# First norm of a decoder layer summed without passes between, and ten modulation blocks at other places of the order

## The chip, the cores and the metric

The kernel runs on one core of a Trainium2 chip. The metric is the device time of one execution in microseconds, as a median of several runs. Times inside an execution are read from a profile of one execution; they count from the start of its span. The engines are named as in the profile: PE is the matmul engine (TensorE), PEld its weight loads, DVE the vector engine, ACT the scalar engine, POOL GpSimd, and SP the engine from whose queue the loads of this kernel are issued (SPq).

## What is computed

One layer of a hybrid decoder, for 256 tokens of width 1024, in float32. A vector `c` gives six modulation vectors; the token mixer (attention of 8 heads beside an SSD group of 16 heads) and a convolutional FFN follow, each behind an RMS norm:

```python
mod = jax.nn.silu(c) @ w_ada[l] + b_ada[l]
shift1, scale1, gate1, shift2, scale2, gate2 = (
    m[:, None, :] for m in jnp.split(mod, N_MOD, axis=-1))
h = rms_norm(x, norm1_g[l]) * (1 + scale1) + shift1
x = x + gate1 * hybrid_token_mixer(h, ...)
h = rms_norm(x, norm2_g[l]) * (1 + scale2) + shift2
x = x + gate2 * conv_ffn(h, ...)
```

In the mixer one projection of `h` gives q, k, v, z, x/B/C and dt. q and k are normed for each head; the attention is causal softmax over the 256 tokens; the SSD group is one chunk of 256 with its decays, a skip and a gate by `silu(z)`. Each group's output is normed, and one output projection takes both.

## The kernel before

**Matmuls.** A weight chunk of 128 rows arrives as `raw` and is split into a high part `whi` (L189, mostly ACT) and a low part `wlo` (L191, mostly DVE). An activation has such parts too (`hhi` and `hlo`, `yhi` and `ylo`, `ahi` and `alo`). A product is then three matmuls: high by high, low weight by high, high weight by low activation. These are L419 in the first stage, L828 to L830 in the stage of z, q, k and v, and L345 to L347 in the output projection and the FFN. L826 multiplies an unsplit chunk.

**The first norm.** Eight tiles `sq` of squares are summed over the features by one-column matmuls against `ones` (L276, two halves of the tokens each, into bank 7; the matmul of a float32 tile shows as two passes in the trace). The square root (ACT, L279) and the reciprocal (DVE, L281) follow, and two transposes (L300) lay the factors along the row that `hbuf` (L385) multiplies. `hhi` (L392) and `h` (L394) come from that, and then the first L419. `keep_warm` (L305) multiplies `ones` by `ones` into a bank that nobody reads; it stands between the sums (`fill`), behind them and behind the transposes. `between()` is `modulate1`: the first two modulation blocks on DVE.

**Modulation.** The product with `w_ada` is made of 48 blocks: each is a load `ada` of 512 KB and, for blocks 0 to 39, one multiply with a running sum on DVE (`ada_dve`, L246). For blocks 16 to 39 the list `ada_u`, sorted, gives the unit of work at which a block stands. It sets two places at once, that of the block's load in SP's queue (behind weight chunk unit + 4) and that of its L246:

```python
ada_unit = sorted(P["ada_u"])
ada_after = [N1 + u + P["ada_lead"] for u in ada_unit] + ...
...
for i in range(16, 40):
    u = ada_unit[i - 16]
    put(u, ada_dve, i)
```

Three `ada` tiles go round for these blocks, so a load waits in the queue until the block three before it has been used, and what stands behind it in SP's queue waits too.

**Units.** A unit is a weight chunk of the second part of the kernel: 0 to 4 are z, 5 to 28 q, k and v, 29 to 44 the output projection. At fixed units stand the conv and dt work, the SSD heads (`ssd_y`: L602 and L603 on PE for a pair of heads, then L604 and L606 on DVE; the decays `m` are L584 to L591), the q and k norms (`rqk` L290 to L296, `qk` L662, transposes L668, `kT` L674), the attention heads (scores L683 and L684, softmax L689 to L705, transposes L711 to L713, the product with v L719 and L720, its parts `ahi` L722 and `alo` L724), the sums for the norms of the groups (L611) and the normed SSD output (`hbuf` L629, `yhi` L630, `ylo` L631).

**Order.** The order of SP is the one written. On PE, DVE and ACT a scheduler with costs of its own orders the instructions from the units, so a change of the list moves many others. Each of these engines then works through its list as it stands: an instruction that waits holds up what is behind it on its engine.

Of the kernel before, what the change touches and what calls it, by code (L numbers as in the profile page):

```python
# [16 lines left out]
D = 1024  # L17
# [24 lines left out]
V_DTB = 326  # L42
V_ALL = 327

P = {'n2l': 6, 'sqa': 0, 'xr0': 0, 'scp': 1, 'vq': 1, 'v1': 6, 'n2': 4, 'hpx': [1, 0, 1, 0, 0, 1], 'e0': 0, 'ev': [1, 0, 1, 0], 'ada_u': [3, 4, 5, 5, 6, 7, 10, 9, 9, 19, 20, 20, 22, 24, 24, 25, 33, 35, 36, 37, 39, 39, 41, 42], 'ada_e': [1, 1, 1, 1, 1, 1, 1, 1, 1, 1, 1, 1, 1, 1, 1, 1, 1, 1, 1, 1, 1, 1, 1, 1], 'ada_lead': 4, 'ada_s': 0, 'g2': 68, 'hip': [0, 0, 0, 0, 0, 0, 0, 0, 0, 0, 0, 0, 0, 0, 0, 0, 0, 0, 0, 0, 0, 0, 0, 0, 0, 0, 0, 0, 0, 0, 1, 0, 0, 0, 1, 0, 0, 0, 0, 1, 0, 0, 0, 0, 0, 0, 0, 0, 0, 0, 0, 0, 0, 0, 0, 0, 0, 0, 0, 0], 'conv': [0, 0, 1, 0, 2, 5, 5, 4, 8, 4, 7, 6], 'dt': [1, 2, 2, 4], 'cdb': [7, 7], 'xbt': [9, 12, 11, 12], 'Y0': 14, 'DL': 3, 'ab0': 11, 'ss': 9, 'so': 2, 'qk': [12, 14, 17, 20, 21, 23], 'A0': 21, 'so1': 2, 'so2': 3, 'pv0': 26, 'sm_e': [0, 0, 1, 0, 1, 0, 0, 0], 'dc_e': [2, 2, 2, 0, 2, 2, 2, 0, 2, 2, 2, 0, 2, 2, 2, 0], 'mm_e': [1, 1, 1, 1, 1, 1, 1, 1, 1, 1, 1, 1, 1, 1, 1, 1], 'gz_e': [0, 0, 0, 0, 0, 0, 0, 0], 'sq_e': [1, 1, 1, 1, 1, 1, 1, 1], 'final': 2, 'ab_q': 0, 'LA': 2, 'asu': 34, 'aru': 38, 'aod': 2, 'w0': 4, 'w1': 4, 'w2': 4, 's1la': -1, 'zi': 1, 'lop': [0, 0, 0, 0, 0, 0, 0, 0, 0, 0, 0, 0, 0, 0, 0, 0, 0, 0, 0, 0, 0, 0, 0, 0, 0, 0, 0, 0, 0, 0, 0, 0, 0, 0, 0, 0, 0, 0, 0, 0, 0, 0, 0, 0, 0, 0, 0, 0, 0, 0, 0, 0, 0, 0, 0, 0, 0, 0, 0, 0], 'subs': [2, 1, 1, 1, 1, 1, 1, 1, 1, 1, 1, 1, 1, 1, 1, 1], 's1a': [0, 1, 0, 1, 0, 0, 0, 0]}

@with_exitstack
def mixer_ffn(ctx: ExitStack, tc: tile.TileContext, xT_d, c_d, vec_d, alog_d, ada_d,
# [22 lines left out]
    bank = [ps.tile([128, 512], F32, name=f"bank{i}") for i in range(8)]  # L71


    RAW, HL, ADA, LA = 8, 5, 3, P["LA"]
# [162 lines left out]
    sq8 = T([128, KT, S], "sq8", tag="big_x")  # L237
# [33 lines left out]
    def rms_sum(parts, n, pb, between=lambda: None, fill=None):  # L271
        for i, p in enumerate(parts):
            if fill and i % 2:
                keep_warm(fill, bank[2][:, 0:128])
            for t in range(2):
                pe.matmul(pb[:, t:t + 1], p[:, t * 128:(t + 1) * 128], ones[:, 0:1], start=(i == t == 0),  # L276
                          stop=(i == len(parts) - 1), skip_group_check=True)
        r = rt()
        act.activation(r[:, 2:4], pb[:, 0:2], AF.Sqrt, bias=epsc, scale=1.0 / n)  # L279
        between()  # L280
        dve.reciprocal(r[:, 0:2], r[:, 2:4])  # L281
        return r
# [15 lines left out]
    def rms_transpose(r, pb):  # L298
        for t in range(2):
            i = pe.transpose(pb[:, 256 + t * 128:384 + t * 128], r[:, t:t + 1].to_broadcast([128, 128]), ident)  # L300
        return i

    def keep_warm(n, out):
        for _ in range(n):
            pe.matmul(out, ones, ones, start=True, stop=True)  # L305
# [30 lines left out]
        ada_dve(1)  # L336

    keep_warm(4, bank[2][:, 0:128])
    r1 = rms_sum([sq8[:, kt] for kt in (0, 1, 2, 3, 4, 6, 5, 7)], D, bank[7], modulate1, 1)
    keep_warm(2, bank[2][:, 0:128])  # L340
    rms_transpose(r1, bank[7])
    keep_warm(5, bank[2][:, 0:128])

    def mm3(out, w, h, start, stop):
        pe.matmul(out, w[0], h[0], start=start, stop=False, skip_group_check=True)  # L345
# [85 lines left out]
    for kt in range(KT):  # L431
        if kt == 0:
# [5 lines left out]
            w0 = get(0)  # L438
# [310 lines left out]
    Y0, DL = P["Y0"], P["DL"]  # L749
# [21 lines left out]
    A0 = P["A0"]  # L771
# [40 lines left out]
    for j in range(6):  # L812
        m, hf = divmod(j, 2)
        bs = (bank[4], bank[6]) if j % 2 else (bank[5], bank[7])
        for q4 in range(4):
# [3 lines left out]
            for k2 in range(2):  # L819
                kt = q4 * 2 + k2 + (m == 2)  # L820
# [244 lines left out]
```

## Time and profile before

| | us |
|---|---|
| median of the runs | 430.8 (430.69, 430.8, 431.64) |
| profiled execution | 430.68 |
| its span, first to last instruction | 429.0 |
| PE busy | 422.5 |
| DVE busy | 344.4 |
| ACT busy | 268.2 |
| POOL busy | 26.0 |

The profiled execution is 1.7 us longer than its span. The busy time of an engine is a sum over the whole span. PE's waits and the timeline of a stretch say where something is late: a row of a timeline has the start, the duration, the engine, the line, the operation, output and inputs, the count of instructions that it holds, and, where the engine stood idle before it, how long and for what. Durations of matmuls overlap, since they are pipelined; the pace of the matmuls is read from one start to the next.

### The profile page before, as it was taken

Reading aid. Unit: us, or ns where it says so; the run is one execution under the profiler, and the core shown is the slowest. Engines: PE = TensorE matmul, PEld = TensorE weight load, DVE = VectorE, ACT = ScalarE, POOL = GpSimd, SP = SyncE. Lnnn points to the kernel's source line nnn. Section 1 sums busy time; section 2 is a strip of 40 time slices with the busy share of each in tenths; the row PEclk is TensorE's granted clock in tenths of the full one; section 3 lists DMA queues with packets and bytes.
Section 4 is the critical chain, followed back from the end, with each engine's and each line's share of the span. In section 5 each row is a group of like instructions: output and inputs, shape, how many; then the busy total and the mean of one; then the engine's idle time right before and its main releaser. Section 6 shows DMA issues by size and latency. Waiting matters only on the chain.

```text
span 429.0 us, 7921 instructions
## 1 busy us (share of the span) xinstructions
PE 422.5 (98%) x3020; PEld 385.1 (90%) x3020; DVE 344.4 (80%) x680; ACT 268.2 (63%) x534; POOL 26.0 (6%) x24
## 2 busy tenths in 40 slices
PE   8999999999999999999999999999999999999996
PEld 8899998768767567889999999999999999999996
DVE  4779968999659888999999699778787877777755
ACT  4375448826999775886267495576666655555640
POOL 2000000000000001000000000222332200000000
PEclk9899999999999999999999999999999999999999
DMA  7999965889359549234691468767776665554002
GB/s 270 398 414 408 388 195 179 306 313 339 103 178 384 185 150 377 100 136 165 232 348 55 136 249 278 270 219 257 261 244 207 236 197 198 161 185 148 0 2 98
DMA packets 29589, 96.19 MB, mean 224 GB/s; under 512 B 3680, under 2 KB 6128, under 8 KB 29552
## 3 DMA queue, kind: packets, MB, share of 16 engines
q1 hardware_dynamic: 29520, 95.68, 62.5%
q8 instruction: 23, 0.38, 0.4%
q14 instruction: 14, 0.11, 0.1%
q10 hardware_dynamic: 32, 0.02, 0.0%
HBM read 94.62 MB, written 1.06 MB: 223 GB/s over the span
## 4 chain that ended last, share of the span: by engine, by line
PE 78%; DVE 9%; DMA 6%; ACT 5%; issue 1%; SPq 1%; ACTq 0%
PE bank L347 17%; PE bank L345 17%; PE bank L346 17%; PE bank L826 4%; PE bank L805 4%; PE bank L828 4%; DMA raw<-in_win_dram 4%; PE bank L829 4%; PE bank L830 4%; DVE wlo L191 2%; DMA vec<-in_vec_dram 2%; ACT whi L189 2%; DVE adax L246 2%; PE bank L931 2%; DVE ada L246 1%; PE bank L419 1%
## 5 line engine op out<-in xcount | busy, mean ns | idle before, releaser
L191 DVE TENSOR_TENSOR wlo<-raw,whi 128x1024 fp32r<-128x1024 f32 (+2 forms) x115 | 143.0, 1245 | 13.8 <-ACT whi L189 13.6
L189 ACT ACTIVATE whi<-raw 128x1024 fp32r<-128x1024 f32 (+2 forms) x112 | 115.0, 1035 | 40.8 <-PE bank L347 30.3
L347 PE MATMUL bank<-h2lo,whi 128*128 128x256 f32 x336 | 95.2, 283 | 0.0
L345 PE MATMUL bank<-h2hi,whi 128*128 128x256 f32 x336 | 95.2, 283 | 0.0
L346 PE MATMUL bank<-h2hi,wlo 128*128 128x256 f32 x336 | 95.1, 283 | 0.0
L916 DVE SCALAR_TENSOR_TENSOR fbuf<-bank,vec,fbuf 128x255 f32<-128x255 f32 (+1 forms) x84 | 40.2, 481 | 30.7 <-ACT fbuf L914 29.3
L347 PEld LDWEIGHTS bank<-h2lo,whi 128*128 128x128 f32 x336 | 64.5, 192 | 0.2 <-DVE h2lo L900 0.2
L345 PEld LDWEIGHTS bank<-h2hi,whi 128*128 128x128 f32 x336 | 64.5, 192 | 0.1
L346 PEld LDWEIGHTS bank<-h2hi,wlo 128*128 128x128 f32 x336 | 64.5, 192 | 0.0
L345 PE MATMUL bank<-fsp,whi 128*128 128x256 f32 x176 | 49.8, 283 | 0.0
L346 PE MATMUL bank<-fsp,wlo 128*128 128x256 f32 x176 | 49.8, 283 | 0.0
L347 PE MATMUL bank<-fsp,whi 128*128 128x256 f32 x176 | 49.8, 283 | 0.0
L914 ACT ACTIVATE fbuf<-bank,vec 128x256 f32<-128x256 f32 x42 | 23.4, 560 | 35.0 <-PE bank L347 35.0
L246 DVE SCALAR_TENSOR_TENSOR ada<-ada,cb 128x1024 f32<-128x1024 f32 x30 | 36.5, 1216 | 0.6 <-DMA ada<-in_ada_dram 0.6
L345 PEld LDWEIGHTS bank<-fsp,whi 128*128 128x128 f32 x176 | 33.8, 192 | 0.0
L346 PEld LDWEIGHTS bank<-fsp,wlo 128*128 128x128 f32 x176 | 33.8, 192 | 0.0
L347 PEld LDWEIGHTS bank<-fsp,whi 128*128 128x128 f32 x176 | 33.8, 192 | 0.0
L828 PE MATMUL bank<-whi,hhi 128*128 128x512 f32 x70 | 29.7, 429 | 0.0
L829 PE MATMUL bank<-wlo,hhi 128*128 128x512 f32 x70 | 28.9, 412 | 0.0
L830 PE MATMUL bank<-whi,hlo 128*128 128x512 f32 x70 | 28.3, 404 | 0.0
L251 POOL TENSOR_TENSOR ada<-ada,cb 128x1024 f32<-128x1024 f32 x8 | 19.8, 2474 | 114.9 <-DMA ada<-in_ada_dram 114.9
L419 PE MATMUL bank<-hhi,whi 128*128 128x256 f32 (+1 forms) x128 | 21.5, 292 | 0.0
(223 smaller groups left out, 830.9 us busy)
## 6 DMA issues: line engine op xcount, KB each, us to landing
raw<-in_wup_dram SPq DMA_DIRECT2D x44, 512.0 KB, 4.3
ada<-in_ada_dram SPq DMA_DIRECT2D x38, 512.0 KB, 5.3
raw<-in_wdn_dram SPq DMA_DIRECT2D x22, 512.0 KB, 3.7
raw<-in_winq_dram SPq DMA_DIRECT2D x16, 512.0 KB, 4.3
raw<-in_wout_dram SPq DMA_DIRECT2D x16, 512.0 KB, 4.7
adax<-in_ada_dram SPq DMA_DIRECT2D x10, 512.0 KB, 9.4
raw<-in_win_dram SPq DMA_DIRECT2D x8, 456.0 KB, 9.8
raw<-in_win_dram SPq DMA_DIRECT2D x7, 512.0 KB, 9.8
```

Source lines behind the costliest of these rows:

```text
L189: act.activation(hi[:, c], t[:, c], AF.Copy)
L191: (pool if lo_on_pool(i) else dve).tensor_tensor(lo[:, c], t[:, c], hi[:, c].bitcast(F32), op=OP.subtract)
L246: dve.scalar_tensor_tensor(t, t, 1.0, sc, op0=OP.mult, op1=OP.mult, accum_out=mod[:, i:i + 1])
L345: pe.matmul(out, w[0], h[0], start=start, stop=False, skip_group_check=True)
L346: pe.matmul(out, w[1], h[0], start=False, stop=False, skip_group_check=True)
L347: pe.matmul(out, w[0], h[1], start=False, stop=stop, skip_group_check=True)
L419: pe.matmul(s1_acc(i)[:m], w[k % 2], h[k // 2], start=(kt == k == 0 and i in (0, 2, 4, 6, 8, 10, 13, 14)), stop=last and kt == KT - 1, ski ...
L828: pe.matmul(bs[t], hhi[:, kt, blk(t)], w[0][:, wc], start=(q4 == k2 == 0), stop=False)
L829: pe.matmul(bs[t], hhi[:, kt, blk(t)], w[1][:, wc], start=False, stop=False)
L830: pe.matmul(bs[t], hlo[:, kt, blk(t)], w[0][:, wc], start=False, stop=(kt == KT - 1))
L914: act.activation(a, src, AF.Identity, bias=vec[:, V_FB + i:V_FB + i + 1], scale=vec[:, w + 2:w + 3])
L916: dve.scalar_tensor_tensor(a[:, s:], src[:, :S - s], vec[:, w + 2 - s:w + 3 - s], a[:, s:], op0=OP.mult, op1=OP.add)
```

## The change

Two edits. In the first norm the sums run without `keep_warm` between them; the two calls behind the sums become seven, and the five behind the transposes become two. In the list `ada_u` (sorted) ten numbers are smaller: blocks 25 to 34 stood at units 19, 20, 20, 22, 24, 24, 25, 33, 35, 36 and now stand at 12, 13, 15, 17, 19, 20, 20, 22, 24, 25; block 35 goes from 37 to 33, block 36 from 39 to 37. Blocks 16 to 24 and 37 to 39 stay.

```diff
-    'ada_u': [3, 4, 5, 5, 6, 7, 10, 9, 9, 19, 20, 20, 22, 24, 24, 25, 33, 35, 36, 37, 39, 39, 41, 42]
+    'ada_u': [3, 4, 5, 5, 6, 7, 9, 9, 10, 12, 13, 15, 17, 19, 20, 20, 22, 24, 25, 33, 37, 39, 41, 42]
...
     keep_warm(4, bank[2][:, 0:128])
-    r1 = rms_sum([sq8[:, kt] for kt in (0, 1, 2, 3, 4, 6, 5, 7)], D, bank[7], modulate1, 1)
+    r1 = rms_sum([sq8[:, kt] for kt in (0, 1, 2, 3, 4, 6, 5, 7)], D, bank[7], modulate1)
+    keep_warm(7, bank[2][:, 0:128])
+    rms_transpose(r1, bank[7])
     keep_warm(2, bank[2][:, 0:128])
-    rms_transpose(r1, bank[7])
-    keep_warm(5, bank[2][:, 0:128])
```

On PE, at the first norm, the last rows of the sums and what follows them (`bank_72` takes the sums and the transposes, `rt` is the square root's tile):

```order
-L276 MATMUL bank_72<-ones,sq_158 128x1 x4
-L305 MATMUL bank_67<-ones 128x128
-L276 MATMUL bank_72<-ones,sq_158 128x1 x2
+L276 MATMUL bank_72<-ones,sq_158 128x1 x16
+L305 MATMUL bank_67<-ones 128x128 x7
+L300 MATMUL bank_72<-ident,rt_173 128x128 x2
 L305 MATMUL bank_67<-ones 128x128 x2
-L300 MATMUL bank_72<-ident,rt_173 128x128 x2
-L305 MATMUL bank_67<-ones 128x128 x5
```

All 16 sums stand in a row, and seven passes of `ones` instead of two stand between them and the transposes.

On DVE, in the q and k part, where the low half of chunk `whi_83` is made (`wlo_88`). `bank_68` holds the result of L602 and L603 for a pair of SSD heads. Before:

```order
L290 TENSOR_SCALAR nw_178<-ssq 128x24
L606 TENSOR_TENSOR xsT<-xsT,zs 128x256
L191 TENSOR_TENSOR wlo_88<-raw_77,whi_83 128x1024
L315 TENSOR_TENSOR accg_788<-accg_788,sq_172 128x256
L291 TENSOR_SCALAR nwi<-nw_178 128x24
L191 TENSOR_TENSOR wlo_89<-raw_79,whi_84 128x1024
L292 TENSOR_SCALAR rqk<-nwi 128x24
L604 SCALAR_TENSOR_TENSOR xsT<-xsT,vec,bank_68 128x256
```

and after:

```order
L290 TENSOR_SCALAR nw_178<-ssq 128x24
L291 TENSOR_SCALAR nwi<-nw_178 128x24
L292 TENSOR_SCALAR rqk<-nwi 128x24
L294 TENSOR_TENSOR nw_179<-rqk 128x24
L295 SCALAR_TENSOR_TENSOR nw_179<-nw_179,nw_178 128x24
L604 SCALAR_TENSOR_TENSOR xsT<-xsT,vec,bank_68 128x256
L191 TENSOR_TENSOR wlo_88<-raw_77,whi_83 128x1024
L315 TENSOR_TENSOR accg_786<-accg_786,sq_172 128x256
```

L604 stood five rows behind `wlo_88` and now stands right ahead of it. On PE the same place reads after the change:

```order
L602 MATMUL bank_68<-m_784,xdt 64x256
L603 MATMUL bank_68<-m_784,xdt 64x128
L828 MATMUL bank_69<-whi_83,hhi 128x512
L828 MATMUL bank_71<-whi_83,hhi 128x512
L829 MATMUL bank_69<-wlo_88,hhi 128x512
L830 MATMUL bank_69<-whi_83,hlo 128x512
```

The pair of heads whose L603 ends two matmuls ahead of the first use of `wlo_88` is the one that L604 above waits for; before, three L828 stood between.

On PE, at the start of the output projection, the second L719 (second head) and what is ahead of it. Before:

```order
L347 MATMUL bank_69<-ylo,whi_85 128x256
L345 MATMUL bank_70<-yhi,whi_82 128x256
L346 MATMUL bank_70<-yhi,wlo_87 128x256
L347 MATMUL bank_70<-ylo,whi_82 128x256
L711 MATMUL bank_67<-ident,p_1463 128x128
L719 MATMUL bank_68<-pT_798,vS 128x256
L720 MATMUL bank_68<-pT_798,vS 128x128
```

and after, with the first L345 of the kernel in the first row:

```order
L345 MATMUL bank_70<-yhi,whi_82 128x256
L683 MATMUL bank_65<-kT,qT 128x128
L684 MATMUL bank_65<-kT,qT 128x256
L711 MATMUL bank_67<-ident,p_1472 128x128
L345 MATMUL bank_69<-yhi,whi_85 128x256
L346 MATMUL bank_69<-yhi,wlo_90 128x256
L711 MATMUL bank_67<-ident,p_1472 128x128 x2
L719 MATMUL bank_68<-pT_796,vS 128x256
L720 MATMUL bank_68<-pT_796,vS 128x128
```

Before, 14 of the L345 stood ahead of this L719; now it is two.

## Rows read from the trace of the kernel before

**Rows 1.** The page, busy time, share of the span and instructions of each engine

```profile
PE 422.5 (98%) x3020; PEld 385.1 (90%) x3020; DVE 344.4 (80%) x680; ACT 268.2 (63%) x534; POOL 26.0 (6%) x24
```

**Rows 2.** Waits of PE: engine, line, releaser, us in total, times, longest

```profile
...
PE bank L668 <- ACT qk L662: 0.4, 1, 0.4
PE bank L611 <- DVE alo L724: 0.4, 1, 0.4
PE bank L719 <- DVE alo L724: 0.3, 1, 0.3
```

**Rows 3.** Timeline of the first norm: start, us, engine, line and operation, count

```profile
10.67 0.47 PE L305 MATMUL bank<-ones 128*128 128x128 f32 x2
...
11.34 0.93 PE L305 MATMUL bank<-ones 128*128 128x128 f32 x4
...
12.06 0.65 PE L300 MATMUL bank<-ident,rt 128*128 128x128 f32 x2
...
12.51 2.34 PE L305 MATMUL bank<-ones 128*128 128x128 f32 x10
...
12.76 0.42 DVE L385 TENSOR_TENSOR hbuf<-xT,bank 128x256 f32<-128x256 f32 x1 [0.60 <-PE bank L300]
...
13.21 0.60 ACT L392 ACTIVATE hhi<-hbuf,mod,gcol 128x256 fp32r<-128x256 f32 x1 [0.92 <-DVE hbuf L385]
...
14.51 1.44 PE L419 MATMUL bank<-hhi,whi 128*128 128x256 f32 x8
```

**Rows 4.** Windows: us, PE, PEld, DVE, ACT, POOL busy, granted clock, DMA, GB/s

```profile
11.50:12.00 0.50, 0.50 (x4) 0.48 (x4) 0.19 (x2) 0.49 (x2) 0.00 (x0) 0.64 1.04 393
12.00:13.00 1.00, 1.00 (x7) 0.97 (x6) 0.40 (x3) 0.29 (x1) 0.00 (x0) 0.50 1.01 408
```

**Rows 5.** Windows, the same columns, in the q and k part

```profile
110.00:120.00 10.00, 10.00 (x47) 6.37 (x46) 4.84 (x13) 9.97 (x34) 0.00 (x0) 1.00 0.23 54
```

**Rows 6.** Timeline of SP's loads and of ACT, q and k part

```profile
92.48 9.74 SPq L146 DMA_DIRECT2D raw<-in_winq_dram  x6
...
107.55 1.06 ACT L189 ACTIVATE whi<-raw 128x1024 fp32r<-128x1024 f32 x1 [2.16 <-PE bank L830]
```

**Rows 7.** Timeline, L604 behind the L603 of an SSD pair

```profile
124.67 0.50 PE L828 MATMUL bank<-whi,hhi 128*128 128x512 f32 x1
...
124.85 0.48 DVE L604 SCALAR_TENSOR_TENSOR xsT<-xsT,vec,bank 128x256 f32<-128x256 f32 x1 [1.44 <-PE bank L603]
```

**Rows 8.** Timelines of DVE and PE where `wlo_88` is made and used

```profile
134.50 1.21 DVE L191 TENSOR_TENSOR wlo<-raw,whi 128x1024 fp32r<-128x1024 f32 x1
...
136.83 0.39 PE L829 MATMUL bank<-wlo,hhi 128*128 128x512 f32 x1
...
137.77 0.39 PE L828 MATMUL bank<-whi,hhi 128*128 128x512 f32 x1
...
138.46 0.39 PE L828 MATMUL bank<-whi,hhi 128*128 128x512 f32 x1
```

**Rows 9.** Timelines of DVE and PE around the last transposes of k

```profile
160.45 1.22 DVE L246 SCALAR_TENSOR_TENSOR ada<-ada,cb 128x1024 f32<-128x1024 f32 x1
...
164.99 0.62 PE L668 MATMUL bank<-ident,qk 128*128 128x128 f32 x2 [0.44 <-ACT qk L662]
```

**Rows 10.** Timeline of DVE: first L629, first and last `alo`

```profile
174.36 1.27 DVE L629 SCALAR_TENSOR_TENSOR hbuf<-xsT,vec,rssm 128x256 f32<-128x256 f32 x3
...
182.97 0.48 DVE L724 SCALAR_TENSOR_TENSOR alo<-bank,vec,ahi 128x256 fp32r<-128x256 f32 x1 [0.25 <-ACT accs L313]
...
204.68 0.47 DVE L724 SCALAR_TENSOR_TENSOR alo<-bank,vec,ahi 128x256 fp32r<-128x256 f32 x1
```

**Rows 11.** Timeline of PE up to the attention's L611

```profile
202.78 0.28 PE L346 MATMUL bank<-yhi,wlo 128*128 128x256 f32 x1
...
204.54 0.28 PE L346 MATMUL bank<-yhi,wlo 128*128 128x256 f32 x1
205.20 0.60 PE L611 MATMUL bank<-ones,accs 128*128 128x1 f32 x4 [0.38 <-DVE alo L724]
```

## What the change will do to the time, predicted from the trace

> **What bounds the kernel now.** I read the first part of the page, then TensorE's waits, then the stretches that the change touches as timelines. The matmul engine is busy for 98% of the span [rows 1], so time comes off only where it stands still, or where it runs at half clock. It waits for few things; two of them concern this change [rows 2]: L668 for ACT's `qk`, 0.4 us, and L611 for DVE's `alo`, 0.4 us. The other place is the start: the granted clock fell within the half microsecond from 11.5 and was 0.50 after it [rows 4], the 1.2 GHz level, just where the first norm's passes and transposes run. Everything behind the first norm is a backlog on TensorE, so a shift of L419 or a wait in the q, k, v stage moves the end by as much, unless a later wait takes it up.
>
> **Part 1, the first norm.** *Removed:* four L305 calls between the sums, two passes each. Six passes, two of L305 and four of L276, take 11.34 - 10.67 = 0.67 us [rows 3], 0.112 each at full clock. Eight fewer are 0.90 us: the sums end, and the L305 behind them start, at 10.44 instead of 11.34. *Added:* seven L305 calls, 14 passes, now stand ahead of the transposes L300 (four passes before). All at full clock they would end at 10.44 + 14 x 0.112 = 12.01, against 12.06 for L300 before [rows 3]. At half clock a pass takes 0.20 (ten from 12.51 to 14.51 [rows 3]). If the clock falls where it fell, at 11.64, some 11 passes run at full and 3 at half rate: 12.27, 0.2 later. If it falls once the sums end, all 14 run at half rate: 13.24, 1.2 later. So the square root and the reciprocal end earlier, and this gains nothing: L300 waits behind the passes on its own engine.
>
> *Behind L300:* `hbuf` comes 0.70 after the transposes, `hhi` ends 1.05 after that [rows 3], and only then can L419 start. Before, L419 started at 14.51 behind the ten L305 passes while `hhi` had ended at 13.81, so 0.7 us stood in hand; with four passes instead of ten this is free. The first L419 can start at 14.0, but the split of the weights on ACT and DVE behind `hhi` and `h` moves with L300 by 0.2, and the second third of the group waits for that. Full clock throughout would give -0.3 (the last L300 and the L419 at the faster rate too), the fall as before +0.1, the early fall up to +1.2. I take **+0.1**, the case nearest to the row: half rate from 11.64.
>
> The PE column is full in every one of those slices, and the clock still fell in the slice 11.5 to 12 [rows 4]; what stood ahead were one-column sums with L305 pairs between. The Trainium skill's page "TensorE: Matmul & The Clock Gate", Part 1, says that the clock is throttled by default and that recent busyness of the engine releases it. [...]
>
> **Part 2, the modulation blocks.** A block is one L246 of 1.22 us on DVE [rows 9] and one load. Ten blocks that stood at units 19 to 37 move up to units 12 to 25; blocks 35 and 36 move by four and two.
> *Where they go:* DVE is busy for 4.84 of the 10 us from 110 to 120 [rows 5]; three or four blocks fit there at no cost. Without that room each would cost 1.2 us, since TensorE waits for `m` and `wlo` there.
> *Their loads:* three now stand in SP's queue among the winq weights and wait for a free buffer. Those six weights left SP from 92.48 to 102.2; the last may leave 1.5 us later. The split at 107.55 waited 2.16 us for TensorE, not for its weight [rows 6]. So nothing.
> *A new wait:* in DVE's new order `wlo_88` stands right behind L604, which waits for the last L603 of its pair of heads; L829 with `wlo_88` stands two matmuls behind that L603 on TensorE. L604 starts 0.18 after the next L828 (124.67, 124.85 [rows 7]), the next instruction 0.40 after that, and `wlo` takes 1.21 [rows 8]: L829 could start 1.84 after that L828, and TensorE reaches it after two passes of 0.23 (three take 138.46 - 137.77 = 0.69 [rows 8]), with switching 0.58. That is **1.26 us** of standing still. Before, this `wlo` was ready at 135.71 and L829 ran at 136.83 [rows 8]. What is queued behind it on DVE (`accg`, `rqk`) comes no later, since L604 moved and not they.
> *A wait that goes:* the second half of kT, L668, stood still at 164.99 for ACT's `qk`, which waited for `rqk`; block 31 lay in that DVE chain at 160.45 [rows 9]. It is no longer there: 0.4 to 0.8 gone, I take 0.6. The 0.54 us at L611 (204.54 + 0.12 to 205.20 [rows 11]) may go too.
> *Attention:* the largest move. In the new TensorE order five groups of L828 to L830 less stand ahead of the second pair of transposes L300, 5 x 0.69 = 3.5 us, and the eight `hbuf` of L629 follow those: instead of 174.36 [rows 10] they start at 174.36 - 3.5 + (1.26 - 0.6) = 171.5. The first `alo` came 8.6 us later (182.97), the last 21.7 after that (204.68), L611 0.5 later [rows 10, 11]. In the new order the same two L246 lie between the first and the last `alo`, and three more short instructions, 0.42 each by the nearest row (L629 x3, 1.27 [rows 10]). At this pace L611 starts at 171.5 + 8.6 + 22.9 + 0.5 = 203.5. But ahead of it now stand 33 fewer passes of L345 to L347, which come behind it: 15 take 1.76 [rows 11], so 33 are 3.9. Counted at equal work that is 203.5 + 3.9 - 205.2 = +2.2. The stall stands ahead of the second L719, which waits for the first head's `alo` near 180: instead of 14 groups of L345 to L347 only two precede it, and the 12 others, 36 x 0.117 = 4.2 us of work, no longer fill that time.
> If DVE loses its idle time on the way, and TensorE alone sets L611, the sum of the single waits holds: 1.26 - 0.6 - 0.54 = +0.1. The rows leave open how much of DVE's waiting vanishes when TensorE runs ahead; I take the middle, **+1.0**, for all of part 2, bounds -1.2 (no new wait at all) and +2.2.
> *Behind 206 us* two blocks fewer remain for DVE, but L611's is the latest of the rows of waits [rows 2]: nothing.
>
> **The sum.** The profiled execution took 430.68 us, its span was 429.0, and the 1.7 around it stay. 430.68 + 0.1 + 1.0 = 431.8 us. The median of the runs, 430.8, lies 0.1 above the profiled one. 0.2% of it, 0.86 us, is about what a measurement of this kernel tells from no change: "same" is 429.9 to 431.7.
>
> **The rivals.**
> *No net change:* TensorE sets L611. For it: before, DVE's part of that wait was only 0.38 [rows 11]. Against it: TensorE's order took out the work that covered the first heads. +0.1 + 0.1: 430.9.
> *Faster:* the wait at `wlo_88` does not come, because L603 of that pair runs with time in hand or DVE's queue is ahead, and the two old waits go: 430.68 - 0.3 - 1.1 = 429.3. It decides where `wlo_88` is done before the two L828 have run. For it: DVE was ready 1.1 us early there before. Against it: the order, in which L604 now stands ahead.
> *The clock falls earlier:* the sums without passes between them bring the half rate at 10.4 or before. The 14 passes then cost 1.2 more, and each sum pass that falls under it 0.09: with ten of them +2.1, so 432.9 to 433.8 with part 2. It decides from the first sums on. For it: the fall at 11.64 came behind these sums. Against it: by 11.64 about as many L305 passes have run as before, only later.
>
> **How the numbers follow.** The forecast, 431.8 us with its own spread from 430.9 to 432.9: 0.37. No net change: 0.28. Faster: 0.22. The early fall: 0.13. The range from 429.1 to 433.4 leaves out some two fifths of the faster case and half of the early fall, some 0.15 together. Faster by over 0.2%: 0.22 and a little of the second case, 0.24. Slower: 0.25 of the forecast, the early fall and a little of the second, 0.41. Within: the rest, 0.35.
>
> **What would show it.** The sums in one row until about 10.5, L300 between 12.0 and 12.3, granted clock 0.50 from 11.6; L300 later than 12.6 means an early fall. DVE between 110 and 127 with three or four L246. TensorE waiting about 1 us at L829 for DVE's `wlo` near 137: if it doesn't, the faster case. No wait at the L668 near 164. A wait of 3 to 5 us ahead of the second L719, ending near 180, and L611 near 203: a wait of under 2 us there, with L611 near 201, means no net change. A wait for a raw weight or an `ada` load near 100 to 108 us would show the loads mispriced, and the forecast wrong in its ground.

## The result and the profile after

The changed kernel takes **436.91 us** (median of 4 runs, 436.36 to 437.14), the kernel before 430.91 in the same comparison: a ratio of 1.0129, 95% interval 1.0116 to 1.0141. The forecast was 431.8 with a range of 429.1 to 433.4. Slower was the likeliest sign, but of 6.0 us the prediction had 1.1. The profiled execution took 436.76 us, its span 435.0.

Busy times on the page of after, as [rows 1]:

```profile
PE 423.4 (97%) x3016; PEld 385.3 (89%) x3016; DVE 350.1 (80%) x680; ACT 268.2 (62%) x534; POOL 24.9 (6%) x24
```

PE's work is the same, its span 6 us longer. Its waits, as [rows 2] (engine, line, releaser, us in total, times, longest):

```profile
PE bank L683 <- ACT p L694: 2.0, 1, 2.0
PE bank L602 <- DVE m L591: 1.2, 1, 1.2
...
PE bank L829 <- DVE wlo L191: 1.1, 1, 1.1
```

The two waits of before that were to go, L668 and L611, are gone. The one foretold at L829 is there. The first two were foretold nowhere at this size, and the three together are 4.3 us, not 6.0.

**Where the time went.** I counted TensorE's work in both traces (every matmul by the usual distance from its start to the next one's, the passes of `ones` at the first norm left out) and compared when each kernel had done the same amount. The lag of after is -0.04 us behind the first norm, +2.77 where before is at 130.9 us, +3.78 at 171.7, +6.09 at the end. The lag stops growing at about 195 us; from there the two run nearly level. So there are four stages to explain: the norm, 37 to 131 us (all of it behind 104), 131 to 172, and the attention. The border at 171.7 us lies among work that the two kernels do in a different order, so the split of the last two stages depends on the distances that the count is made with: with the median distance over all traces it is 0.60 and 2.71 instead of 1.01 and 2.31. The first two stages and the sum do not move.

*The first norm*, as [rows 3, 4], timeline and windows of after:

```profile
10.71 1.81 PE L305 MATMUL bank<-ones 128*128 128x128 f32 x14
12.36 0.38 PE L300 MATMUL bank<-ident,rt 128*128 128x128 f32 x2
...
13.88 0.74 PE L419 MATMUL bank<-hhi,whi 128*128 128x256 f32 x4 [0.70 <-ACT hhi L392]
```

```profile
11.50:12.00 0.50, 0.50 (x7) 0.50 (x6) 0.03 (x1) 0.17 (x1) 0.00 (x0) 1.00 1.04 397
12.00:13.00 1.00, 1.00 (x11) 0.99 (x9) 0.23 (x1) 0.00 (x0) 0.00 (x0) 1.00 1.04 413
```

The transposes come at 12.36, 0.3 later than before. The granted clock stays 1.00 here; the lateness comes from a first sum that starts at 7.22 instead of 6.95 us. L419 gains back what the transposes lost.

*Up to 131 us.* SP's loads, of before and then of after (start, us of issuing, queue, line, tile and source, count; from 92.4 us on, the last row of each as far as 118 us):

```profile
92.48 9.74 SPq L146 DMA_DIRECT2D raw<-in_winq_dram  x6
104.19 0.33 SPq L146 DMA_DIRECT2D raw<-in_winv_dram  x1
104.56 9.88 SPq L578 DMA_DIRECT2D ab<-acd  x8
```

```profile
92.47 1.54 SPq L146 DMA_DIRECT2D raw<-in_winq_dram  x2
98.62 0.33 SPq L152 DMA_DIRECT2D ada<-in_ada_dram  x1
99.04 0.39 SPq L146 DMA_DIRECT2D raw<-in_winq_dram  x1
100.75 0.33 SPq L152 DMA_DIRECT2D ada<-in_ada_dram  x1
101.17 1.21 SPq L146 DMA_DIRECT2D raw<-in_winq_dram  x2
103.03 0.33 SPq L152 DMA_DIRECT2D ada<-in_ada_dram  x1
103.45 0.66 SPq L146 DMA_DIRECT2D raw<-in_winq_dram  x1
104.20 0.43 SPq L146 DMA_DIRECT2D raw<-in_winv_dram  x1
104.68 11.24 SPq L578 DMA_DIRECT2D ab<-acd  x5
```

Three loads of blocks (25, 26, 27) now stand among the weights. The queue stands from 94.0 to 98.62, until block 22 gives its tile free. The weights still come in time, since ACT's split at 107.53 waits 2.16 for PE as in [rows 6]. But behind them stand the small loads `ab` (L578, 128 KB each): the rows from which the decays `m` of the SSD heads are made (L584 on ACT, L591 on DVE, then L602 and L603 on PE). The first four are issued at almost the same time in both kernels, from 104.56 and from 104.68, but land at 109.2 to 110.1 before and at 113.8 to 114.8 after, behind the blocks. ACT's first L584, before and after:

```profile
109.19 0.51 ACT L584 ACTIVATE m<-ab,acum 128x256 f32<-128x256 f32 x1
```

```profile
110.92 0.60 ACT L644 ACTIVATE qk<-bank 128x512 f32<-128x512 f32 x1 [1.85 <-PE bank L830]
...
114.78 0.51 ACT L584 ACTIVATE m<-ab,acum 128x256 f32<-128x256 f32 x1
```

In the new order of ACT two L644, a second L672, a split and five L648 stand ahead of it. On PE the first L602 comes at 119.05 instead of 114.76, and this is how two groups of L602 and L603 look there:

```profile
121.48 0.66 PE L602 MATMUL bank<-m,xdt 128*64 128x256 f32 x4
...
125.66 0.65 PE L602 MATMUL bank<-m,xdt 128*64 128x256 f32 x2 [1.24 <-DVE m L591]
...
126.88 0.65 PE L602 MATMUL bank<-m,xdt 128*64 128x256 f32 x2
```

The group at 121.48 is a pair of heads (8 passes, 0.81 us to the next instruction); the one at 125.66 is a single head (4 passes, 0.79): a head alone costs as much as two. With the step into each group, all groups take 10.75 us before, with one pair torn apart, and 12.98 after, with two torn and one wait. The torn pair of before stands behind 131 us. The first five pairs alone, those of this stage, take 5.85 before and 8.86 after, and these 3.0 us are the stage's whole lag: 1.24 of waiting, some 1.3 for the pair torn in two at 125.66 and 126.88, and 0.7 for the first pair, whose passes are mixed (1.30 us instead of 0.81). The wait is that of DVE for a later `ab` row, issued at 119.66 and landed at 124.57:

```profile
124.59 0.35 DVE L588 TENSOR_SCALAR m<-ab,nacum 128x256 f32<-128x256 f32 x1 [1.64 <-DMA ab<-acd]
```

*From 131 to 172 us*, DVE and PE of after, as [rows 7, 8]:

```profile
138.93 0.48 DVE L604 SCALAR_TENSOR_TENSOR xsT<-xsT,vec,bank 128x256 f32<-128x256 f32 x1 [0.70 <-PE bank L603]
139.33 1.22 DVE L191 TENSOR_TENSOR wlo<-raw,whi 128x1024 fp32r<-128x1024 f32 x1
...
140.60 0.50 PE L829 MATMUL bank<-wlo,hhi 128*128 128x512 f32 x1 [1.06 <-DVE wlo L191]
```

This is the wait of the prediction, 0.2 below the size given for it.

*The attention*, timelines of ACT and PE of after, then windows (the columns of [rows 4]); before, 30 passes of L345 to L347 stood between 175.8 and 179.8 us, where only one L345 stands now. ACT first, one row of before and then those of after:

```profile
179.12 0.46 ACT L694 ACTIVATE p<-bank,sm,rqk 128x128 f32<-128x128 f32 x1 [0.92 <-DVE sm L692]
```

```profile
179.20 1.04 ACT L189 ACTIVATE whi<-raw 128x1024 fp32r<-128x1024 f32 x1
180.14 0.45 ACT L694 ACTIVATE p<-bank,sm,rqk 128x128 f32<-128x128 f32 x1
...
180.58 0.56 ACT L694 ACTIVATE p<-bank,sm,rqk 128x256 f32<-128x256 f32 x1
```

PE:

```profile
178.97 0.28 PE L345 MATMUL bank<-yhi,whi 128*128 128x256 f32 x1
181.28 0.49 PE L683 MATMUL bank<-kT,qT 128*128 128x128 f32 x2 [2.04 <-ACT p L694]
```

Windows:

```profile
182.00:183.00 1.00, 0.60 (x4) 0.30 (x3) 1.00 (x4) 1.00 (x4) 0.00 (x0) 0.93 0.00 0
183.00:186.00 3.00, 3.00 (x13) 2.73 (x12) 2.34 (x9) 2.31 (x9) 0.00 (x0) 0.50 0.00 0
```

The scores L683 need the bank from which ACT's L694 reads, and on ACT a split of a weight (L189) stands ahead of it: L694 comes 1.0 later than before. The other 1.0 of the standstill is the cover that is gone. Behind the standstill the granted clock is 0.50, the 1.2 GHz level, for 3 us of full work. The Trainium skill's page "TensorE: Matmul & The Clock Gate", Part 1, says that the clock depends on how busy the engine was shortly before; this row agrees.

### The profile page after: what moved, and what is told of

It is laid out like the page before. It is cut to its first block, busy times and chain, and to the rows that moved or that the text cites. A ratio compares the mean times of both kernels' runs of the same rounds, so it can differ in the third digit from the quotient of the medians.

```text
span 435.0 us, 7912 instructions
## 1 busy us (share of the span) xinstructions
PE 423.4 (97%) x3016; PEld 385.3 (89%) x3016; DVE 350.1 (80%) x680; ACT 268.2 (62%) x534; POOL 24.9 (6%) x24
## 3 DMA queue, kind: packets, MB, share of 16 engines
HBM read 94.62 MB, written 1.06 MB: 220 GB/s over the span
## 4 chain that ended last, share of the span: by engine, by line
PE 79%; DVE 12%; ACT 6%; issue 1%; DMA 1%; SPq 0%; POOL 0%; ACTq 0%; POOLq 0%
PE bank L347 17%; PE bank L345 17%; PE bank L346 17%; PE bank L805 4%; PE bank L826 4%; DVE wlo L191 3%; PE bank L829 3%; PE bank L830 3%; PE bank L828 3%; DVE adax L246 2%; PE bank L419 2%; ACT whi L189 2%; PE bank L931 2%; DVE ada L246 1%; DMA ab<-acd 1%
## 5 line engine op out<-in xcount | busy, mean ns | idle before, releaser
L191 DVE TENSOR_TENSOR wlo<-raw,whi 128x1024 fp32r<-128x1024 f32 (+2 forms) x115 | 145.1, 1263 | 15.8 <-ACT whi L189 15.5
L189 ACT ACTIVATE whi<-raw 128x1024 fp32r<-128x1024 f32 (+2 forms) x112 | 114.8, 1035 | 39.2 <-PE bank L347 26.4
L347 PE MATMUL bank<-h2lo,whi 128*128 128x256 f32 x336 | 95.2, 283 | 0.0
L345 PE MATMUL bank<-h2hi,whi 128*128 128x256 f32 x336 | 95.2, 283 | 0.0
L347 PEld LDWEIGHTS bank<-h2lo,whi 128*128 128x128 f32 x336 | 64.5, 192 | 0.2 <-DVE h2lo L900 0.2
L345 PEld LDWEIGHTS bank<-h2hi,whi 128*128 128x128 f32 x336 | 64.5, 192 | 0.1
L345 PE MATMUL bank<-fsp,whi 128*128 128x256 f32 x176 | 49.8, 283 | 0.0
L347 PE MATMUL bank<-fsp,whi 128*128 128x256 f32 x176 | 49.8, 283 | 0.0
L246 DVE SCALAR_TENSOR_TENSOR ada<-ada,cb 128x1024 f32<-128x1024 f32 x30 | 36.5, 1216 | 0.6 <-DMA ada<-in_ada_dram 0.6
L345 PEld LDWEIGHTS bank<-fsp,whi 128*128 128x128 f32 x176 | 33.8, 192 | 0.0
L347 PEld LDWEIGHTS bank<-fsp,whi 128*128 128x128 f32 x176 | 33.8, 192 | 0.0
L829 PE MATMUL bank<-wlo,hhi 128*128 128x512 f32 x70 | 28.2, 403 | 1.1 <-DVE wlo L191 1.1
L828 PE MATMUL bank<-whi,hhi 128*128 128x512 f32 x70 | 28.9, 415 | 0.0
L419 PE MATMUL bank<-hhi,whi 128*128 128x256 f32 (+1 forms) x128 | 21.5, 290 | 1.3 <-ACT hhi L392 0.7
```

Source lines behind the costliest of these rows:

```text
L189: act.activation(hi[:, c], t[:, c], AF.Copy)
L191: (pool if lo_on_pool(i) else dve).tensor_tensor(lo[:, c], t[:, c], hi[:, c].bitcast(F32), op=OP.subtract)
L246: dve.scalar_tensor_tensor(t, t, 1.0, sc, op0=OP.mult, op1=OP.mult, accum_out=mod[:, i:i + 1])
L347: pe.matmul(out, w[0], h[1], start=False, stop=stop, skip_group_check=True)
L419: pe.matmul(s1_acc(i)[:m], w[k % 2], h[k // 2], start=(kt == k == 0 and i in (0, 2, 4, 6, 8, 10, 13, 14)), stop=last and kt == KT - 1, ski ...
L828: pe.matmul(bs[t], hhi[:, kt, blk(t)], w[0][:, wc], start=(q4 == k2 == 0), stop=False)
```

## The experiments

All experiments change the kernel before or after in the places shown. "Old norm" is the first norm of before, "new list" the list `ada_u` of after. The table gives medians and ratios to the kernel before in the same comparison, and the lag as above, split by stage (each from one profiled execution). With the other count the last two columns shift as said, but between kernels with the same order on the engines the differences stay within 0.3. In `spread_pin` the border at 131 us falls on a wait: the other count gives 4.24 and 3.49 for its two middle columns.

| kernel | us | ratio, interval | norm | to 131 | to 172 | to the end |
|---|---|---|---|---|---|---|
| after | 436.91 | 1.0129 [1.0116, 1.0141] | -0.04 | 2.81 | 1.01 | 2.31 |
| norm_only | 431.2 | 1.0002 [0.9987, 1.0016] | 0.36 | 0.05 | -0.01 | 0.16 |
| spread_only | 436.03 | 1.011 [1.0096, 1.0124] | -0.02 | 1.85 | 1.01 | 2.47 |
| after_wlo | 438.62 | 1.0155 [1.0112, 1.0197] | 3.51 | 2.44 | -0.16 | 2.21 |
| after_act | 436.58 | 1.0141 [1.0105, 1.0176] | 0.00 | 1.81 | 1.32 | 0.47 |
| spread_wlo | 434.24 | 1.0071 [1.0046, 1.0096] | 0.60 | 1.65 | 0.08 | 1.83 |
| spread_act | 435.43 | 1.0094 [1.008, 1.0107] | 0.90 | 1.83 | 1.02 | 1.15 |
| spread_wlo_act | 434.68 | 1.0077 [1.0057, 1.0097] | 0.61 | 1.85 | 0.07 | 0.87 |
| spread_pin | 439.55 | 1.019 [1.0173, 1.0207] | 0.62 | 6.24 | 1.54 | 1.14 |
| spread_pin_ab8 | 443.65 | 1.0289 [1.0249, 1.0329] | 0.83 | 7.96 | 5.28 | 1.17 |
| spread_early_ab | 438.07 | 1.0152 [1.0137, 1.0167] | 0.57 | 3.19 | 1.05 | 1.98 |
| spread_early_ab_wlo_act | 437.4 | 1.0142 [1.0125, 1.0158] | 0.60 | 3.88 | 0.08 | 0.68 |
| spread_no_loads | 436.07 | 1.0115 [1.0097, 1.0133] | 0.72 | 2.17 | 1.27 | 0.47 |
| spread_no_loads_wlo_act | 433.89 | 1.0059 [1.0041, 1.0077] | 0.68 | 1.50 | 0.11 | 2.02 |
| spread_no_loads_free | 434.32 | 1.0066 [1.005, 1.0083] | -0.06 | 0.28 | -0.19 | 3.60 |
| spread_pin_no_loads | 438.07 | 1.0151 [1.0135, 1.0166] | 0.01 | 2.20 | 3.97 | 1.27 |
| before_ab8 | 430.91 | 0.9989 [0.998, 0.9999] | 0.79 | 0.04 | -1.08 | 0.50 |
| after_ab8 | 429.69 | 0.9977 [0.9959, 0.9995] | -0.03 | 0.27 | -1.66 | -0.14 |
| spread_ab8 | 428.84 | 0.9947 [0.9934, 0.996] | -0.09 | 0.10 | -1.66 | -0.39 |

### Which half of the change

`norm_only` is after with the old list, `spread_only` before with the new list:

```diff
-    'ada_u': [3, 4, 5, 5, 6, 7, 9, 9, 10, 12, 13, 15, 17, 19, 20, 20, 22, 24, 25, 33, 37, 39, 41, 42]
+    'ada_u': [3, 4, 5, 5, 6, 7, 10, 9, 9, 19, 20, 20, 22, 24, 24, 25, 33, 35, 36, 37, 39, 39, 41, 42]
```

> Only the norm edit; the list of the blocks is that of before, and so is the order of all instructions behind the norm. In the trace of after the first L405 starts 0.05 us earlier than before and everything up to 110 us is level with before. Theory A (part 1 is worth nothing): 430.6 to 431.1 us, within 0.2 us of before. Theory B (part 1 has a share in the 6 us, by a clock that falls at another time in most runs): 432 us or more.

> Only the new list of blocks; the norm is that of before, and the order behind the norm is the one of after, instruction by instruction. Theory A: the whole loss, 436.5 to 437.2 us. Theory B: 2 us or more less than after, under 435 us.

The norm is worth nothing: 431.2 against 431.38. The list costs 436.03 - 431.38 = 4.65 us, between the two ranges written down and nearer to the first. What after loses beyond that lies in the second stage, in the wait at L602: 1.2 us in after, 0.2 in `spread_only`, where the order is the same and the `ab` row of that wait landed at 123.61 instead of 124.57.

### The waits at L829 and L683

`after_wlo` exchanges two neighbours on DVE, `after_act` moves one weight's split on ACT; the rest of the order is held:

```diff
-L604 SCALAR_TENSOR_TENSOR xsT<-xsT,vec,bank_68 128x256
 L191 TENSOR_TENSOR wlo_88<-raw_77,whi_83 128x1024
+L604 SCALAR_TENSOR_TENSOR xsT<-xsT,vec,bank_68 128x256
```

```diff
-L189 ACTIVATE whi_84<-raw_75 128x1024
 L694 ACTIVATE p
 L694 ACTIVATE p
+L189 ACTIVATE whi_84<-raw_75 128x1024
```

> After, in its own order, but with two neighbours on DVE exchanged: the wlo that L829 waits for near 140.6 us stands ahead of the L604 that waits for PE. By the prediction's term the wait of 1.1 to 1.26 us at L829 goes and nothing takes it up: 435.5 to 435.9 us. If a later wait takes it up (the one at L683 near 181 hangs on DVE and ACT), 436.5 us or more.

> After, in its own order, but with the weight split L189 that stands on ACT right ahead of a head's two L694 put behind them; it waits for PE to end with the weight before. L683 near 181 waits for these L694. If ACT's order is the cause of that wait, about 1.0 us of its 2.0 goes, and with it perhaps the clock's fall at 183: 434.3 to 435.9 us. If DVE is (its sm comes no earlier), 436.5 us or more.

The medians alone would have misled: 438.62 and 436.58, both on the side written down against the theory, with single runs from 434.27 to 439.23. For `after_wlo` the rows say why: the clock fell at the first norm and stayed down (windows, columns as in [rows 4]):

```profile
10.00:11.00 1.00, 1.00 (x9) 1.00 (x9) 1.00 (x4) 0.09 (x1) 0.00 (x0) 0.76 1.07 404
...
15.00:16.00 1.00, 1.00 (x6) 1.00 (x6) 0.00 (x0) 0.00 (x0) 0.00 (x0) 0.50 1.00 401
```

That is the 3.51 in its norm column. Its own stage, to 172 us, went from 1.01 to -0.16, as expected. The profiled execution of `after_act` is the fastest of its four runs; what slowed the others is not shown. So I repeated both with the old norm, alone and together:

> New list of blocks, first norm as before, and on VectorE the weight step of wlo_88 (L191) one place earlier, ahead of the one product of L604 that it followed; nothing else moves. Three theories of the 5 us that the new list costs (436.03 against 430.9): decays late, a wait at L829 for wlo_88, a standstill at L683. If the wait at L829 is a term of its own, it goes and the time is 434.6 to 435.1 (1.2 less than 436.03, or a little less, since L603 then waits for L604's buffer). If it only covers another wait, the time stays 435.6 to 436.3. With the norm as before no long runs from the first norm's clock are expected: all runs within 1 us.

> New list of blocks, first norm as before, and on ScalarE the rounding of whi_84 (L189, 1.04 us) two places later, behind the two evictions of L694 that the V state's matmuls wait for; nothing else moves. If PE's 2.0 us at L683 and the half-clock stretch behind it are a term of their own, the wait falls to about 1 us, the granted clock at 183 to 186 us stays 1.00, and the time is 434.0 to 434.9. If the clock falls all the same, 435.0 to 435.4. If the weight that is rounded later makes PE wait in its turn, 435.8 or more.

> Both exchanges together, new list, first norm as before. If the three terms add up, 436.03 less both: 432.9 to 433.7, which leaves 2 to 3 us over the kernel before for the late decays alone. If one wait only takes over from another, 434.5 to 435.5.

Each acts in its own column: the exchange on DVE takes 1.01 to 0.08 or 0.07, the one on ACT 2.47 to 1.15 or 0.87. All three medians lie outside the ranges for a term of its own: `spread_wlo` 0.4 below, `spread_act` half a microsecond above (its norm took 0.90 longer in the profiled run), and the pair together at 434.68 instead of 432.9 to 433.7, in the range written down for a wait that takes over from another. By the medians the exchange on ACT adds nothing to the one on DVE (434.68 against 434.24); by the columns it takes 1.0 more in the attention. The runs of `spread_wlo` lie 3.4 us apart (433.09 to 436.52), not within 1: the norm and the clock behind L683 (below) both vary. So the old norm has such runs as well, only smaller ones. In its rows of waits the pair has half the standstill left, the half that the missing cover makes, and a second one behind it:

```profile
PE bank L683 <- ACT p L694: 1.1, 1, 1.1
...
PE bank L711 <- ACT p L703: 0.6, 1, 0.6
```

### The late decay rows

First, the old order with the new blocks: `spread_pin` holds PE and ACT to the order of before, and DVE too but for the moved L246. Such a kernel gives each engine a fixed list and lets each instruction follow the one ahead of it:

```diff
-    order = tc.manual_schedule()
+    order = tc.manual_schedule(engines={mybir.EngineType.Pool})
...
+    pin()
```

> The new list, but the order of PE, DVE and ACT is held to that of before, except that each moved L246 stands on DVE behind the same weight split as in after; the loads stand in SP's queue as in after. Theory 1 (the loss comes from the new order, with L829 waiting for wlo and the first heads late): no wait at L829 near 137, L668 still late or not, 430 to 432 us. Theory 2 (the loss comes from the moved loads, which push the ab rows of the decays from 109.2 to 113.8 us): L602 stands still for about 4 us near 115 to 120, 434 us or more.

```profile
114.81 0.51 ACT L584 ACTIVATE m<-ab,acum 128x256 f32<-128x256 f32 x1 [5.09 <-DMA ab<-acd]
```

ACT now waits 5.09 us for the row that in before was there at 109.19: the rows are late, whatever the order. Then `after_ab8` brings them forward: `ab0` is the unit at which the first four `ab` loads stand in SP's queue. `before_ab8` does the same to the kernel before, `spread_pin_ab8` to `spread_pin`:

```diff
-    'ab0': 11
+    'ab0': 8
```

> After, with the first four ab loads three units earlier, so that they stand in SP's queue ahead of the loads of blocks 25 to 27; the order is planned anew from there on. Theory 2 (late ab rows): the first L584 runs near 109 instead of 114.8 us, the 1.3 us wait of L602 on m at 125.7 goes, 432 to 434.5 us. Theory 1: 436 us or more, unless the new order happens to avoid the waits at L829 and L683.

> Before, with the first four ab loads three units earlier; planned anew from there. If after_ab8 gained on before because the ab rows come early, this gains as much: 429 to 430 us. If it gained because the moved blocks fill DVE's idle time, this stays at 431 to 431.6 us.

> The held order of spread_pin on PE, DVE and ACT, row for row; alone the first four ab loads stand earlier in SP's queue, ahead of the loads of blocks 25 to 27. In spread_pin ACT stood still for 5.1 us at the first L584 for its ab row, and PE 1.7 us and more at L602. Theory 2 (late ab rows): the ab rows land near 102, ACT's wait goes, 433 to 435.5 us (what is left are waits at L568 and L668 for xdt, behind the L246 rows that were put in by hand). Theory 1 (it is the order): 438.5 us or more.

`after_ab8` is 7.2 us faster than after and 0.23% faster than before; `before_ab8` gains at most 0.2%, and its 430.91 lies between its two ranges. But `spread_pin_ab8` lies 8 us above what late rows alone would give, on the side written down for the order: ACT's wait is gone, and the blocks, now behind the rows, are late themselves (DVE):

```profile
108.26 1.23 DVE L246 SCALAR_TENSOR_TENSOR ada<-ada,cb 128x1024 f32<-128x1024 f32 x1 [3.25 <-DMA ada<-in_ada_dram]
...
109.41 0.69 DVE L569 TENSOR_TENSOR xdt<-bank,dtc 128x512 f32<-128x512 f32 x1
```

Behind that L246 stands `xdt`, for which PE waits at L568, L668 and L602. `after_ab8` differs from after in the order of every engine, so it doesn't say which part of this helped. `spread_early_ab` changes SP's queue alone, with the order of `spread_only` held:

> New list of blocks, first norm as before, the order of TensorE, VectorE and ScalarE held to the one the new list gave (436.03), and only SP's queue changed: the first four loads of decay rows (L578) ahead of the loads of blocks 25 to 27. after_ab8 did this too, but there the scheduler laid the other engines out anew. If late decay rows are 2.8 us of the loss and the waits at L829 and L683 terms of their own, 432.8 to 433.6, with both waits still in the rows of waits at about 1.1 and 2.0. If those two waits follow from the late rows as well, 430 to 431.5 and they shrink or go. If the later block loads now hold L246 and with it xdt (as in spread_pin_ab8), 435 or more.

> The same with both exchanges of neighbours (wlo_88 ahead of one L604, whi_84 behind two L694). If the three causes make up the whole loss, it is at the time of the kernel before, 430.2 to 431.6. If something of the new list is left unexplained, 432 or more. If the exchanges only displace a wait once the rows are early, as spread_early_ab or less than 0.5 below it.

Both are slower than `spread_only`. The first is the third of its outcomes; the second has 0.67 less than the first, a little more than its third outcome allows. The rows come early, and in their place ACT waits 3.34 us for a raw weight at 109.29 and L246 for its block (DVE):

```profile
107.95 1.22 DVE L246 SCALAR_TENSOR_TENSOR ada<-ada,cb 128x1024 f32<-128x1024 f32 x1 [1.94 <-DMA ada<-in_ada_dram]
```

So with this order some user of the queue is late whichever goes first. Is it the loads, then, or L246 on DVE? `spread_no_loads` leaves the three loads out and holds the order; `spread_no_loads_free` lets the scheduler lay the order out again; `spread_pin_no_loads` holds the order of before:

```diff
-                sp.dma_start(t, ada_d[i])
+                i in (25, 26, 27) or sp.dma_start(t, ada_d[i])
...
-        dve.scalar_tensor_tensor(t, t, 1.0, sc,
+        dve.scalar_tensor_tensor(t, sc if i in (25, 26, 27) else t, 1.0, sc,
```

> spread_only's kernel with its order of TensorE, VectorE and ScalarE held, and the three loads of blocks 25, 26 and 27 left out of SP's queue. Their L246 stay where they are and as long, but read the table cb in place of the block, so these three columns of mod are not computed and the output is not the reference's. spread_early_ab was slower (438.07), since the block loads, now later, held L246 and a raw weight held ScalarE: some user of the queue is late whichever goes first. If the three loads between 92 and 108 us are what costs the 2.8 us, the decay rows land by 106 to 110 and TensorE is level with the kernel before until 127: 432.7 to 433.6 if the waits at L829 and L683 are terms of their own, 430 to 431.5 if they follow from the loads too. If it is VectorE's L246 among the other work that costs, nothing changes: 435.5 to 436.3.

> The same (columns 25 to 27 of mod not computed) with both exchanges of neighbours (wlo_88 ahead of one L604, whi_84 behind two L694). If loads, L829 and L683 together are the whole loss: 430.0 to 431.3, the time of the kernel before. If something is left unexplained, 432 or more.

My theory that the loads cost by being late fell with `spread_no_loads`: without them and with the order held, stage two still lags by 2.17. The second run fell with it: 433.89 instead of 430.0 to 431.3, with 1.50 left in stage two and the clock down behind L683. The order is what costs in stage two. ACT has L584 behind L644, L644 waits for PE, and the groups of L602 stay torn: the first five pairs take 8.23 us. ACT's first L584, whose row landed at 109.86 here:

```profile
115.52 0.51 ACT L584 ACTIVATE m<-ab,acum 128x256 f32<-128x256 f32 x1
```

> As spread_no_loads (loads of blocks 25 to 27 left out, their L246 read cb, so columns 25 to 27 of mod are not computed), but the order of the engines is laid out anew by the scheduler instead of held. ScalarE's row then has its first L584 right behind the first qT (L672) again, as in the kernel before, where the new list with its loads had put L644, L189 and four L648 ahead. If the loads cost through the order that the scheduler chooses around late rows, the decays start near 109, the groups of L602 are whole again, and the time is 429.5 to 431.5. If L246 on VectorE are the cost, or the loads had nothing to do with it, 434 or more, as spread_no_loads.

> As spread_pin (order of TensorE and ScalarE held to the kernel before's, VectorE's too but for the moved L246), with the loads of blocks 25 to 27 left out (columns 25 to 27 of mod not computed). spread_pin took 439.55: 5.1 us of waiting for decay rows on ScalarE, then waits at L602, L568 and L668. If these all come from the loads, the rows land as in the kernel before and the time is 430.5 to 432.5. If the L246 put by hand among xdt cost of themselves, 433 to 436, with waits of L568 for xdt left.

With the order laid out anew, ACT's list has L584 right behind the first L672 again, the first five pairs take 6.08 us, and the lag of stage two is 0.28, of stage three -0.19. In `after_ab8`, where the loads stay and the rows go ahead of them, the five pairs take 5.87. So the loads cost through the order: where the rows land late, the scheduler lays the decays behind other work. What it reckons with is not seen, only the order that it makes. The whole of 434.32 - 431.45 = 2.9 us that is left lies in the attention: waits of 2.1 at L683 and 1.1 at L719 (0.6 and 0.3 before), 0.4 at L711, and the clock at 0.50 behind the first. That is why the expectation of 429.5 to 431.5 missed: I had taken the standstill at L683 for a matter of some 1 us, and the column has 3.6. `spread_pin_no_loads` missed too: in the order of before the L246 of the left-out blocks, put by hand right ahead of `xdt`, hold PE by themselves (0.7 at L568, 1.1 at L668). Its wait of 2.6 at L602 is another matter: there an L246 waits 2.06 for the load of a later block. Free time of DVE in a stretch does not make every place in it free.

### The standstill and the clock

Seven profiled executions have a wait of 2.0 to 2.1 us at L683. In six the granted clock then fell to 0.50, the 1.2 GHz level, for some 3 us; their last column is 1.8 to 3.6. In `spread_no_loads` it stayed 1.00, and the last column is 0.47. Of five with a wait of 1.1, one fell (`spread_no_loads_wlo_act`, 2.02); the others have 0.47 to 1.15. Without the wait (`after_ab8`, `spread_ab8`), or with the 0.6 us of the kernel before, the clock stayed up. So the column has some 0.5 to 1 us where there is a standstill alone (1.1 to 1.6 with the other count), and about 1.5 more where the clock falls. These are single executions, and that PE waits less behind a long standstill is a guess from the columns.

### The best version

`spread_ab8` joins the new list and early rows with the old norm:

> New list of blocks, decay rows loaded ahead of the loads of blocks 25 to 27 (as in after_ab8, same order behind the first norm), first norm as before. after_ab8 had a median of 429.69 with two runs of ten near 432.4. If these came from the first norm's sums without passes between (half clock beyond the sums, as norm_only and after_wlo show it in single runs), all runs here lie at 429.3 to 430.5. If they come from the order behind, one run in five is near 432 here too. Against the kernel before (430.9 to 431.4): ratio 0.995 to 0.998.

428.84 us, 0.53% faster than before and 8 us faster than after: faster than expected, and its five runs have none near 432.4, of which `after_ab8` has two in ten; five runs are few to tell. Its rows of waits hold no L829, L683 or L602:

```profile
PE bank L719 <- DVE alo L724: 1.6, 2, 1.2
PE bank L229 <- POOL ones L227: 1.1, 1, 1.1
```

All eight groups of L602 and L603 are whole pairs, 9.50 us in all against 10.75 before; that is 1.25 of the 1.66 us it gains between 131 and 172. With the old list `before_ab8` has whole groups too (9.88), so most of this comes from the early rows and not from the moved blocks.

## Why the prediction was wrong, step by step

**Part 1, +0.1: the size right, the path by luck.** The kernel with this edit alone is level with before. The transposes came at 12.36 (foretold 12.0 to 12.3, and later than 12.6 for an early fall), but not because the clock fell at 11.6: in the profiled execution it did not fall there at all, and full clock was to give -0.3. The sums had started 0.27 later. In other executions the clock did fall: the third rival, the early fall, is real in some, at 3.5 us in the worst one seen.

**The loads, "so nothing": the step that failed.** It asked whether the weights come in time, and they do; its 1.5 us for the last of them is right too (103.45 instead of 101.90). It did not ask what stands behind the weights in the same queue, and its view of SP's loads [rows 6] ended just ahead of the `ab` rows. Moving three loads of 512 KB ahead of four of 128 KB made those land 4.6 us later, and with that the scheduler made another order. The prediction went by the new order on PE and DVE at the norm, near 138 us and in the attention, but not by ACT's and PE's from 108 to 131 us. Measured: 1.85 to 2.81 us up to 131 us; gone (0.28) where the loads are left out and the order is laid out anew. The sentence at the end of the prediction, on a wait for a raw weight or an `ada` load, named the right queue and the wrong tile.

**DVE's room, "nothing": not contradicted in the order that the scheduler chose, and hardly tested.** DVE is busy for 7.09 of the 10 us from 110 to 120 [rows 5] without PE waiting for an L246, but only one L246 stands there, and two from 110 to 127 instead of the three or four foretold. It is not right for any place: the same blocks by hand cost 2.2 us by 113.

**The wait at L829, +1.26: right.** 1.06 of waiting, and the exchange that removes it takes 1.17 out of its stage. (The three terms, 0.18, 0.40 and 1.21, add up to 1.79 and not 1.84, so the sum should have read 1.21.) **L668 and L611, both to go: right.**

**Attention: the second step that failed, with the mechanism right and the place and the size wrong.** The +0.1, the +2.2 and the middle are for all of part 2; less the 1.26 and with the 0.6 they leave some 0.3 for the attention, at most 1.5. The cover was taken away as described, but the stall came at L683 for ACT's L694, not at the second L719 for `alo`: I followed DVE's chain and not the one that needs ACT, where a weight's split stood in the way and made half of the wait. Behind the standstill the clock fell, which no term had. Measured 2.31 (2.71 by the other count).

**The sum.** -0.04 + 2.81 + 1.01 + 2.31 = 6.09, against 0.1 + 1.0. Some 2.8 of the missing 5 us are the loads, and some 2 the attention: the standstill with its clock. The rivals held none of this: all of them kept the loads at nothing.

## What to carry to other kernels

When a load moves forward in a queue, list everything that is behind its new place up to its old one, the small loads above all, and ask for each who waits for it. Where a scheduler lays out the engines, a load that lands late can come back as another order on all of them, and that order costs even when the load is then on time. Compare the new order of every engine with the old one over the whole stretch, not only at the places that the change names. Taking filler work away from ahead of a wait costs twice where the clock falls behind the wait.

## What the runs showed of the hardware

**A head alone costs as much as a pair.** The matmuls L602 and L603 write 64 of the 128 rows of a bank: a pair of heads side by side takes 0.81 us, with the passes of the two heads starting 0.014 us apart, and one head with other matmuls behind it 0.79. The Trainium skill's page "TensorE: Matmul & The Clock Gate", Part 3 (on packing small matmuls), says that small matmuls in different parts of the array can run at once; these rows agree, and show that another matmul between the two undoes it.

**The half-rate stretch at the first norm differs between executions of the same norm.** With the changed norm it was absent (after), some 3 us long (`norm_only`) or longer than 6 us (`after_wlo`); with the old norm the stage varied by 0.9. For changes of less than 1% a median over few runs can point the wrong way; the lag by stage, though from one execution each, showed in which stage the difference lay.
